# A hybrid decoder trunk on one core: five accumulator banks in its last gate, pool products by 64 by 64 blocks, and a new order of all instructions

## Chip, cores and metric

The kernel runs on one core of a Trainium2 chip. The metric is the device time of one execution in microseconds (us); less is better. A profile is one execution of the same program, taken by the hardware profiler. The engines are called as in the profile: PE (matrix products), PEld (its weight loads), DVE (vector), ACT (activations), POOL (GpSimd) and SP (which only issues DMAs here).

## What is computed

Two layers (L = 2) over 256 tokens and 1024 features, all in float32. `z` is split by columns among a convolution module, a pooling mixer, and a sparse attention that keeps 64 keys per query; each is multiplied by a SiLU gate. Then come an output projection, a residual, and an addition gated by a sigmoid. A last RMSNorm ends it.

```python
for i in range(DEPTH):
    n = rmsnorm(h, norm_g[i])
    z = n @ w_in[i] + b_in[i]
    ...
    ya = conv_module(c_val, c_glu, ...) * jax.nn.silu(c_gate)
    yb = pool_mixer(p_in, pool_w[i], pool_b[i], pool_scale[i]) * jax.nn.silu(p_gate)
    ...
    yc = sparse_attention(q, k, v, qi, ki, wi) * jax.nn.silu(a_gate)
    h = h + jnp.concatenate([ya, yb, yc], axis=-1) @ w_out[i]
    h = h + (p[i] @ ple_w[i]) * jax.nn.sigmoid(h @ ple_gate_w[i])
return rmsnorm(h, final_norm_g)
```

In the pooling mixer each of four groups of 64 channels is multiplied by its own 64 by 64 matrix: `jnp.einsum('bsgc,gcd->bsgd', d, w)`.

## The kernel before

**Products.** Features lie on the 128 partitions, tokens in the free dimension. Every large weight arrives by DMA in one of three buffers `raw` (1 MB each). ACT or DVE rounds it to `hi`, DVE or POOL subtracts to get `lo`, and a product is three passes on PE: hi times hi, hi times lo, lo times hi. The sum of eight such k-steps stays in a PSUM bank. There are eight banks of 512 columns; `bank()` hands out banks 0 to 2 in turn, `bank("att")` banks 4 to 7. Small products (index scores, attention, pooling, convolution's pointwise part) are taken in float32 directly.

**Order.** The program text only records operations, each with the engines that may do it. `Order.issue` then issues them in the order of the string `ORDER`: two characters per operation, which say which operation comes next and which engine takes it. `PORT` adds waits between a few operations of POOL and DVE. Each engine works through its own part of that order strictly in a row, SP its DMAs too. A PSUM bank counts as one cell: whoever writes any part of it waits for all that read or write it.

**Places of which the prediction speaks.** (1) In `rope_pair` the projected `z` has its partitions swapped by four DMAs `zs<-z`, issued by SP or ACT; the index scores (`score1`, products `bank<-qir`) need the result, and they need bank 5, which the projection Q0 of layer 1 uses until `rescale` (DVE) and `evac` (ACT) have emptied it. The load of `mt` (mats, 384 KB) stands in SP's queue too. (2) In the convolution's layer norm (`ln`), POOL takes `nyl`, the reciprocal root, DVE makes `nm` of it, and two `c<-bank,nm,nyl` normalise, after which PE transposes them. (3) In the pooling mixer two products by block-diagonal 128 by 128 matrices (`mt`) are made in each layer. (4) In `last_gate` the tokens lie on the partitions; the output of 256 by 1024 is made in five parts (`LAST_PARTS`). Parts 4 and 5 (columns 512 to 767 and 768 to 1023 of the second 128 tokens) share a bank. After a part's products come a sigmoid in place (ACT), the product with `ple` (DVE), the sum with the transposed residual `ht` (DVE), a square with its sum (ACT), and a small step of the variance `nv` (DVE). `ht` comes from PE transposes that ACT copies (`vt<-bank`).

```python
LAST_PARTS = ((0, 0, 512), (0, 512, 512), (1, 0, 512), (1, 512, 256), (1, 768, 256))
```

Of the kernel before, what the change touches and what calls it, by code (L numbers as in the profile page):

```python
# [20 lines left out]
L = 2  # L21
S = 256
# [41 lines left out]
    "#Z#m###j#&#*#p#-%y#0#K#3#N#6%|#9#d#_#Q#<#b#?#B#s#}$##v&##g$B#y$E#W$($3$*$H&*#T$K&&$6&-$Q%3%7&B$T$W$p%:$9&0(9%<"  # L64
    "$<$N$Z%@%B&Q&3$?$.&W%F&6$0#E#H%W%H$a%K$d&9%N&^%Z%R$g&<%_$j%T$s&d$^&?&j%a)3&E&p$v&v&K&H&|$y&N&T(<$m&Z$|)g&a(?%#"
    "&g)<*Q%&&m%*)6)?(B(E(H%d)9%g(K&s%j+<)p%m(N(Q%0&y)j)t%p%s(T(W%w)B(Z(&(#(^*Z(d)E(*(m*T)H*^(s)K(a*W)N(|)Q(-)m.^+?"
    ")T(p(3(0(y)W+C3p(j*a(6+E-s)Z3s*d)^3v*g(h+I3y(w*j)a3|4#*m.a4&*p4*/H*s)$4-40*v.e)v.g*y)y43)d46)|+#)&.j*#*&)*7p49"
    "+K).*|-v4<**+44?*-4B)14E*04H-z+-+N-|*3+0+Q4K+**94N+T*64Q*<+W.#/K%-+Z*B+(/N+^6g*@+a*F4T*I.&4W4Z.*+7+d.-4^+j+g4a"
    "*L.0/Q7g4d.34g6j*O.64j4m.m4p/U.94s.<,&.?,*,y+:8N4v,-,0,3+v-#4y,|,6+p,9/W6n.B4|+s6p,<.p5#,?-&.E5&.s.N.L,B6t.R5*"
    ".v,E.I5-.y--,H7s.|50,K.U9-/#53+n,N/&-*+z/Z/*/^,Q.X/0,T/a7y,W56/d+}8Q,Z6v59,^/-.[/g,a5<6y,d,$-06|,g-37#,j8U/6/:"  # L70
    "-6,m7&90/<5?7*-9/3,p/j,s-<,v/v-?94/y/|/m0&-B0*8^-E0-5B8a-H/@005E-K8d8W/C0#/p030B068g-N0E5H/F090H0<7--Q0?5K70-T"
# [992 lines left out]
```

## Time and profile before

| | us |
|---|---|
| median of 3 runs | 335.52 |
| the three runs | 335.54, 335.52, 333.81 |
| profiled execution, its own time | 334.27 |
| span from first to last instruction | 332.2 |
| PE busy in the span | 315.4 |
| DVE, ACT, POOL busy | 255.0, 181.2, 154.0 |

The profiled execution is 1.25 us under the median, and 2.1 us of it lie outside the span. In rows of the timeline the columns are start, duration, engine, line, operation, what it writes and reads, shapes and count; in brackets the idle time of the engine before it and what ended it. Consecutive equal instructions are merged, and their duration is then that of the row. A duration of a PE product runs past the start of the next one, since products are pipelined; the distance of starts says what one costs.

### The profile page before, as it was taken

What the parts mean: (1) busy time and instruction counts of PE and PEld (TensorE: products, weight loads), DVE (VectorE), ACT (ScalarE), POOL (GpSimd) and SP (SyncE); (2) the same over time, 40 slices, a digit from 0 to 9 for tenths busy, and PEclk for the clock granted to TensorE, in tenths of its full rate; (3) what the DMA queues carried; (4) which work ended last, traced back from release to release, by engine and by line L of the source; (5) the groups of instructions that cost most, each with busy time, mean ns of one, the idle gap of its engine ahead of it and who ended that gap; (6) DMA issues with size and microseconds to landing.
All of it is one profiled execution on the core that took longest, in us unless ns stands there. A gap on an engine that the chain in (4) does not pass through costs nothing. (4 is left out here: it accounts for less than half of the span.)

```text
span 332.2 us, 6467 instructions
## 1 busy us (share of the span) xinstructions
PE 315.4 (95%) x2468; PEld 294.1 (89%) x2469; DVE 255.0 (77%) x570; ACT 181.2 (55%) x319; POOL 154.0 (46%) x109
## 2 busy tenths in 40 slices
PE   8989999898999999999999998999999989999990
PEld 3979999797789999999999998998898979998870
DVE  3887999997786898357997987987798783838373
ACT  2776552628658545252686526536767661533463
POOL 1003577979985000461300463996967655020122
PEclk9999999999999999999999999999999999999997
DMA  7959977461163155626456774372343338351003
GB/s 214 325 190 357 303 271 240 156 228 36 33 247 134 52 202 195 269 77 221 161 144 247 272 236 149 129 257 94 128 132 131 118 117 280 134 215 80 0 0 126
DMA packets 13549, 57.31 MB, mean 173 GB/s; under 512 B 2128, under 2 KB 3280, under 8 KB 8016
## 3 DMA queue, kind: packets, MB, share of 16 engines
q1 hardware_dynamic: 12128, 55.14, 47.6%
q10 hardware_dynamic: 1392, 1.77, 1.8%
q8 instruction: 19, 0.31, 0.4%
q14 instruction: 10, 0.08, 0.1%
HBM read 52.45 MB, written 1.05 MB: 161 GB/s over the span
## 5 line engine op out<-in xcount | busy, mean ns | idle before, releaser
L209 PE MATMUL bank<-xhi,hi 128*128 128x256 f32 x464 | 132.0, 286 | 0.3 <-ACT ple L260 0.2
L209 PE MATMUL bank<-xlo,hi 128*128 128x256 f32 (+1 forms) x464 | 129.7, 281 | 0.5 <-DVE xlo L280 0.5
L209 PE MATMUL bank<-xhi,lo 128*128 128x256 f32 x448 | 125.9, 281 | 2.2 <-POOL lo L282 1.4
L282 POOL TENSOR_TENSOR lo<-raw,hi 128x1024 fp32r<-128x1024 f32 (+1 forms) x40 | 93.6, 2351 | 70.4 <-DVE hi L262 40.1
L260 ACT ACTIVATE hi<-raw 128x1024 fp32r<-128x1024 f32 (+2 forms) x89 | 87.3, 1007 | 54.1 <-PE bank L209 24.4
L209 PEld LDWEIGHTS bank<-xhi,hi 128*128 128x128 f32 x464 | 87.3, 188 | 1.8 <-ACT ple L260 0.4
L209 PEld LDWEIGHTS bank<-xlo,hi 128*128 128x128 f32 (+1 forms) x464 | 86.6, 187 | 1.1 <-DVE xlo L280 0.9
L209 PEld LDWEIGHTS bank<-xhi,lo 128*128 128x128 f32 x448 | 84.5, 189 | 2.8 <-POOL lo L282 1.8
L280 DVE TENSOR_TENSOR lo<-raw,hi 128x1024 fp32r<-128x1024 f32 (+2 forms) x58 | 64.9, 1147 | 9.5 <-ACT hi L260 9.2
L287 DVE SCALAR_TENSOR_TENSOR bank<-f,f,bank 128x256 f32<-128x256 f32 x116 | 55.9, 482 | 1.7
L209 PE MATMUL bank<-yhi,hi 128*128 128x256 f32 x128 | 36.3, 284 | 0.0
L209 PE MATMUL bank<-ylo,hi 128*128 128x256 f32 x128 | 36.1, 282 | 0.0
L209 PE MATMUL bank<-yhi,lo 128*128 128x256 f32 x128 | 35.9, 281 | 0.0
L209 PE MATMUL bank<-hi,xhi 128*128 128x256 f32 (+2 forms) x100 | 32.1, 321 | 0.7 <-DVE vt L270 0.7
L209 PE MATMUL bank<-hi,xlo 128*128 128x256 f32 (+2 forms) x100 | 31.3, 313 | 0.0
L209 PE MATMUL bank<-lo,xhi 128*128 128x256 f32 (+2 forms) x100 | 31.2, 312 | 0.0
L209 PEld LDWEIGHTS bank<-yhi,hi 128*128 128x128 f32 x128 | 24.1, 188 | 0.3 <-DVE c L229 0.2
L209 PEld LDWEIGHTS bank<-ylo,hi 128*128 128x128 f32 x128 | 24.1, 188 | 0.3
L209 PEld LDWEIGHTS bank<-yhi,lo 128*128 128x128 f32 x128 | 24.1, 188 | 0.0
L209 PEld LDWEIGHTS bank<-hi,xhi 128*128 128x128 f32 x100 | 18.8, 188 | 2.9 <-DVE vt L270 0.9
L228 ACT ACTIVATE z<-bank,f 128x256 f32<-128x256 f32 x21 | 9.3, 470 | 20.6 <-DMA zs<-z 9.2
L270 DVE TENSOR_TENSOR bank<-bank,rb 128x512 f32<-128x512 f32 (+1 forms) x26 | 17.3, 672 | 4.0 <-PE bank L209 3.8
(175 smaller groups left out, 470.2 us busy)
## 6 DMA issues: line engine op xcount, KB each, us to landing
raw<-in_w_in_dram SPq DMA_DIRECT2D x25, 1024.0 KB, 6.3
raw<-in_w_out_dram SPq DMA_DIRECT2D x8, 1024.0 KB, 4.8
raw<-in_w_gate_dram SPq DMA_DIRECT2D x8, 1024.0 KB, 5.0
raw<-in_w_v_dram SPq DMA_DIRECT2D x2, 1040.0 KB, 5.3
raw<-in_w_ple_dram SPq DMA_DIRECT2D x8, 256.0 KB, 5.2
zs<-z SPq DMA_DIRECT2D x21, 64.0 KB, 2.2
zs<-z ACTq DMA_DIRECT2D x19, 64.0 KB, 4.0
raw<-in_w_in_dram SPq DMA_DIRECT2D x4, 256.0 KB, 6.3
```

What stands on the lines that cost most here:

```text
L209: lambda: self.nc.tensor.matmul(o, lhsT, rhs, start=start, stop=stop, skip_group_check=True))],
L228: self.add([self.on_act(o, i, lambda: self.nc.scalar.activation(o, i, AF.Identity, bias=bias, **kw), len(ptr)), self.on_dve(o.free_size(), ...
L260: ways.append(self.on_act(o, i, lambda: self.nc.scalar.activation(o, i, AF.Copy)))
L270: ways.append(self.on_dve(n, lambda: self.nc.vector.tensor_tensor(o, a, b, op), late=late))
L280: ways.append(self.on_dve(n, lambda: self.nc.vector.tensor_tensor(o, a, hb, OP.subtract), late=late))
L282: ways.append(self.on_pool(n, lambda: self.nc.gpsimd.tensor_tensor(o, a, hb, OP.subtract)))
L287: self.add([self.on_dve(o.free_size(), lambda: self.nc.vector.scalar_tensor_tensor(o, a, s, b, op0=op0, op1=op1), len(ptr))], [a, b] + ptr ...
```

## The change

Three things. `last_gate` gets a fifth bank, and part 5 accumulates there; its first four k-steps are therefore also made by parts, so that the 512 columns of the second token half are two times 256. Its transposes take their buffers from a list of three banks. The pool products are four of 64 by 64 instead of two of 128 by 128 in each layer. And `ORDER` and `PORT` are replaced as a whole.

```diff
 ORDER = (
-    "#Z#m###j#&#*#p#-%y#0#K#3#N#6%|#9#d#_#Q#<#b#?#B#s#}$##v&##g$B#y$E#W$($3$*$H&*#T$K&&$6$-$Q%3%7&B$T$W$p%:$9&0(9%<"
...
+    "#m#Z###j#&#*#p#-%y#0#N#3#K#6#T#9#}#s$##^#Q#e#a#g%|$B#w$E#y$H$&&#$K#<$+#?&*#W$3$6#B&&$Q%3%7&B$9$O$p$T&-$<%K(9$W"
...
         ppl = bank("att")
         for j in range(2):
-            R.mm(ppl[:, j * S:(j + 1) * S], mt[:, 512 + j * 128:512 + j * 128 + 128], pd[j], start=(j == 0), stop=True)
+            for r in (slice(0, 64), slice(64, 128)):
+                c0 = 512 + j * 128 + r.start
+                R.mm(ppl[r, j * S:(j + 1) * S], mt[r, c0:c0 + 64], pd[j][r], start=(j == 0), stop=True)
...
-            return last_gate(hhi, hlo, ple, [banks[3], bank("att"), bank("att"), bank()])
+            return last_gate(hhi, hlo, ple, [banks[3], bank("att"), bank("att"), bank(), bank()])
...
+        tbs = [bank(), bank("att"), bank("att")]
         for a in range(2):
             for t in range(2):
                 R.tag = f"ht{a}{t}"
-                tb = bank("acc" if a == 0 else "att")
+                tb = tbs[(2 * a + t) % 3]
...
-        halves = ((0, 512), (512, 512))
-        order = [[(k, t, c, n) for k in range(GATE_OUTER) for t in range(2) for c, n in halves]]
+        order = [[(k, *part) for k in range(GATE_OUTER) for part in LAST_PARTS]]
+
+        def acc_of(t, c, n):
+            b, c0 = (accs[4], 768) if (t, c) == (1, 768) else (accs[2 * t + c // 512], c // 512 * 512)
+            return b[:, c - c0:c - c0 + n]
+
```

The new order, at the three places where the prediction uses it:

**The layer norm of layer 1.** DVE before, from the batch statistics of the convolution (`bmv`) to the second normalisation; `bank0` and `bank2` are gates of other branches, `yhi` and `ylo` a split for the output projection.

```order
L767 BN_AGGR bmv65_145<-bst64_144 128x2
L270 TENSOR_TENSOR bank0_61<-bank0_61,y078_158 128x512
L293 TENSOR_SCALAR vv66_146<-bmv65_145 128x2
L262 CAST yhi71_151<-bank0_61 128x512
L280 TENSOR_TENSOR ylo72_152<-bank0_61,yhi71_151 128x512
L287 SCALAR_TENSOR_TENSOR nm70_150<-bmv65_145,nyl67_147 128x2
L270 TENSOR_TENSOR bank2_63<-bank2_63,rb42_122 128x512
L229 TENSOR_SCALAR c269_149<-bank6_67,nyl67_147,nm70_150 128x256
```

And DVE in the changed program:

```order
L766 BN_AGGR bmv65_145<-bst64_144 128x2
L292 TENSOR_SCALAR vv66_146<-bmv65_145 128x2
L269 TENSOR_TENSOR bank0_61<-bank0_61,y078_158 128x512
L286 SCALAR_TENSOR_TENSOR nm70_150<-bmv65_145,nyl67_147 128x2
L261 CAST yhi71_151<-bank0_61 128x512
L279 TENSOR_TENSOR ylo72_152<-bank0_61,yhi71_151 128x512
L269 TENSOR_TENSOR bank2_63<-bank2_63,rb42_122 128x512
```

The step `vv` now stands ahead of the product in bank 0, and `nm` ahead of the split into `yhi` and `ylo`; the second normalisation has left DVE. ACT at the same place, before:

```order
L218 ACT_TABLE_LOAD
L218 ACTIVATE bank0_61<-bank0_61,f3_78 128x256 x2
L260 ACTIVATE hi20_100<-raw17_97 128x1024
L228 ACTIVATE c269_149<-bank6_67,nm70_150,nyl67_147 128x256
L218 ACTIVATE ag79_159<-bank2_63,f3_78 128x256 x2
```

And ACT in the changed program:

```order
L217 ACT_TABLE_LOAD
L217 ACTIVATE bank0_61<-bank0_61,f3_78 128x256 x2
L259 ACTIVATE hi19_99<-raw16_96 128x1024
L259 ACTIVATE hi20_100<-raw17_97 128x1024
L227 ACTIVATE c269_149<-bank6_67,nm70_150,nyl67_147 128x256 x2
L217 ACTIVATE ag79_159<-bank2_63,f3_78 128x256 x2
```

Another rounding (`hi19`) stands ahead of `hi20`, from which POOL subtracts next after `nyl`; both normalisations follow on ACT.

**SP's queue at the index scores of layer 1.** Before (`zs39<-z37` are the swaps for the index queries, `zs38<-z36` with 512 columns those of Q0, `raw` the weights):

```order
L312 DMA z36_116<-z36_116 64x256
L312 DMA zs38_118<-z36_116 32x256 x2
L312 DMA mt33_113<-in_mats_dram 128x768
L312 DMA raw15_95<-in_w_in_dram 128x2048
L312 DMA zs39_119<-z37_117 32x512 x2
L312 DMA raw17_97<-in_w_in_dram 128x2048
L312 DMA zs38_118<-z36_116 32x512 x2
L312 DMA raw16_96<-in_w_in_dram 128x2048
L312 DMA zs38_118<-z36_116 32x512 x2
```

And in the changed program:

```order
L311 DMA raw15_95<-in_w_in_dram 128x2048
L311 DMA zs39_119<-z37_117 32x512 x3
L311 DMA zs38_118<-z36_116 32x512 x2
L311 DMA raw17_97<-in_w_in_dram 128x2048
L311 DMA raw16_96<-in_w_in_dram 128x2048
L311 DMA zs38_118<-z36_116 32x512 x4
L311 DMA raw15_95<-in_w_in_dram 128x2048
L311 DMA zs39_119<-z37_117 32x512
L311 DMA mt33_113<-in_mats_dram 128x768
L311 DMA raw17_97<-in_w_in_dram 128x2048
```

The load of `mt` has moved from ahead of the index queries' swaps to behind many later ones, and the load of raw17 from ahead of Q0's swaps to behind them.

**The end of the last gate.** PE before, from the last products of part 4 (bank 2) over the last transposes (`f0<-f5`) to the first products of part 5, which has the same bank:

```order
L209 MATMUL bank2_63<-hi21_101,xhi34_114 128x256
L209 MATMUL bank2_63<-lo25_105,xhi34_114 128x256
L209 MATMUL bank2_63<-hi21_101,xlo35_115 128x256
L213 MATMUL bank5_66<-f0_69,f5_80 128x128 x3
L213 MATMUL bank1_62<-f0_69,f5_80 128x128 x4
L209 MATMUL bank2_63<-hi18_98,xhi34_114 128x256
L209 MATMUL bank2_63<-lo28_108,xhi34_114 128x256
L209 MATMUL bank2_63<-hi18_98,xlo35_115 128x256
```

And PE in the changed program, with part 5 in bank 0:

```order
L208 MATMUL bank2_63<-hi21_101,xhi34_114 128x256
L208 MATMUL bank2_63<-lo25_105,xhi34_114 128x256
L208 MATMUL bank2_63<-hi21_101,xlo35_115 128x256
L212 MATMUL bank1_62<-f0_69,f5_80 128x128 x4
L212 MATMUL bank4_65<-f0_69,f5_80 128x128 x3
L208 MATMUL bank0_61<-hi18_98,xhi34_114 128x256
L208 MATMUL bank0_61<-lo28_108,xhi34_114 128x256
L208 MATMUL bank0_61<-hi18_98,xlo35_115 128x256
L212 MATMUL bank4_65<-f0_69,f5_80 128x128
L208 MATMUL bank0_61<-hi19_99,xhi34_114 128x256
```

The seven transposes stand at the same place, an eighth has moved behind three products of part 5. ACT before, from the sigmoid of part 4 on:

```order
L218 ACTIVATE bank2_63<-bank2_63 128x256
L260 ACTIVATE vt45_125<-bank5_66 128x512
L260 ACTIVATE vt45_125<-bank1_62 128x512
L298 ACTIVATE q455_135<-q455_135,nyr082_162 128x512
L218 ACTIVATE pTs59_139,ssq80_160<-vt45_125 128x512
L218 ACTIVATE bank2_63<-bank2_63 128x256
L218 ACTIVATE pTs59_139,ssq80_160<-vt45_125 128x256
```

And ACT in the changed program:

```order
L217 ACTIVATE bank2_63<-bank2_63 128x256
L259 ACTIVATE vt45_125<-bank1_62 128x512
L259 ACTIVATE vt45_125<-bank4_65 128x512
L217 ACTIVATE bank0_61<-bank0_61 128x256
L217 ACTIVATE pTs59_139,ssq80_160<-vt45_125 128x512
L217 ACTIVATE pTs59_139,ssq80_160<-vt45_125 128x256 x2
```

The sigmoid of part 5 (bank 0) now stands ahead of the square of part 3 (`pTs,ssq<-vt`, 512 columns). On DVE the first step of `nv1` (which waits for that square) stands ahead of part 5's product with `ple` in both programs.

## Rows read from the trace of the kernel before

**Rows 1.** The page, busy time, share and instructions of each engine.

```profile
PE 315.4 (95%) x2468; PEld 294.1 (89%) x2469; DVE 255.0 (77%) x570; ACT 181.2 (55%) x319; POOL 154.0 (46%) x109
```

**Rows 2.** Waits of PE: releaser, us in total, times, longest.

```profile
PE bank L209 <- POOL qir L272: 1.2, 1, 1.2
PE bank L209 <- ACT z L228: 1.1, 1, 1.1
```

**Rows 3.** Timeline of SP, DVE and ACT before the index scores, layer 1.

```profile
192.81 0.53 SPq L312 DMA_DIRECT2D mt<-in_mats_dram  x1
195.24 1.15 SPq L312 DMA_DIRECT2D zs<-z  x2
...
201.13 0.69 DVE L270 TENSOR_TENSOR zs<-zs,f 128x512 f32<-128x512 f32 x1 [2.72 <-DMA zs<-z]
202.13 0.69 DVE L270 TENSOR_TENSOR bank<-bank,rb 128x512 f32<-128x512 f32 x1
...
202.86 0.84 ACT L228 ACTIVATE z<-bank,f 128x256 f32<-128x256 f32 x2 [0.66 <-DVE bank L270]
```

**Rows 4.** Timeline of DVE, POOL, ACT and PE at the layer norm, layer 1.

```profile
265.84 1.86 DVE L287 SCALAR_TENSOR_TENSOR nm<-bmv,nyl 128x2 f32<-128x2 f32 x1
...
265.28 2.39 POOL L282 TENSOR_TENSOR lo<-raw,hi 128x1024 fp32r<-128x1024 f32 x1
...
263.66 1.05 ACT L260 ACTIVATE hi<-raw 128x1024 fp32r<-128x1024 f32 x1
267.73 0.56 ACT L228 ACTIVATE c<-bank,nm,nyl 128x256 f32<-128x256 f32 x1 [3.02 <-DVE nm L287]
...
267.36 0.28 PE L209 MATMUL bank<-yhi,lo 128*128 128x256 f32 x1
268.35 0.33 PE L213 MATMUL bank<-f,c 128*128 128x128 f32 x1 [0.71 <-ACT c L228]
268.93 0.55 PE L213 MATMUL bank<-f,c 128*128 128x128 f32 x3 [0.25 <-DVE c L229]
```

**Rows 5.** Timeline of PE: pool products of layer 0, and products on half of the rows.

```profile
110.99 0.61 PE L209 MATMUL bank<-pd,mt 128*128 128x256 f32 x2
111.43 0.38 PE L209 MATMUL bank<-c,mt 128*128 128x256 f32 x1
...
86.95 1.14 PE L209 MATMUL bank<-zrk,zrq 64*128 64x256 f32 x8
88.02 0.44 PE L209 MATMUL bank<-pTs,vt 128*64 128x128 f32 x4
```

**Rows 6.** Timeline of PE, ACT and DVE at the end of the last gate.

```profile
321.27 0.93 PE L213 MATMUL bank<-f,f 128*128 128x128 f32 x7
322.91 0.39 PE L209 MATMUL bank<-hi,xhi 128*128 128x256 f32 x1 [0.71 <-DVE vt L270]
324.31 0.28 PE L209 MATMUL bank<-hi,xlo 128*128 128x256 f32 x1
...
323.64 0.64 ACT L218 ACTIVATE pTs<-vt 128x512 f32<-128x512 f32 x1
324.63 0.37 ACT L218 ACTIVATE bank<-bank 128x256 f32<-128x256 f32 x1 [0.26 <-PE bank L209]
...
324.40 0.15 DVE L293 TENSOR_SCALAR nv<-ssq 128x1 f32<-128x1 f32 x1
325.03 0.43 DVE L270 TENSOR_TENSOR bank<-bank,ple 128x256 f32<-128x256 f32 x1 [0.47 <-ACT bank L218]
```

**Rows 7.** Timeline of PE at the start: warm-up products, the first real ones, the last long wait.

```profile
1.25 4.88 PE L209 MATMUL bank<-f 128*128 128x512 bf16 x11 [1.25 <-DVE f L379]
6.03 0.58 PE L209 MATMUL bank<-phi,hi 128*128 128x256 f32 x1
6.41 0.42 PE L209 MATMUL bank<-plo,hi 128*128 128x256 f32 x1
...
21.98 0.38 PE L209 MATMUL bank<-xhi,lo 128*128 128x256 f32 x1 [0.76 <-DVE lo L280]
```

More of the change, by code (lines that the diff above doesn't have):

```diff
@@ new lines @@
+    "(s*a3p(j)W3s(g3v*d+E(a3y*g%-3|(w(d+I*j4#(n(p4&*m.a-s4**p4-(})Z40*s.e/H(z43+K46*v)v.g*y)$)y49)&)|)*.j*|*#+#*&4<"
+    "-v).4?**+44B*-4E*0)1-z+N+*-|*3+-+Q4H*6)a+04K+T+(4N+W/K4Q.#+Z*9+^*B*F/N.&*=6g*@.*4T+74W+a*I.-+d.04Z*L+g4^.3/Q4a"
+    ".64d*O)^.94g)d+j4j.<+:+m4m,*6p+s.?,&,-/U+v4p,|,0,34s.m,64v.E.p,9.B4y/W.L,<6t8T4|.R/Z7v,?6j5#.s,B5&.v.O,E6n+q.y"
+    ",H.I7m,K/^5*,N/a5-,Q.|+}9350,T/#53+z/&,W56,Z,y.X-&59-#,^-*6v/*.U6y,a/0-0--6|,d8W5<,$7#,g/--3,j7&8#.[-6/9,m/d/6"
+    "/45?,p/g8[/<7y-9,s/j-<96/v/y/|0#,v/m-?/C0&-B7*0*-E0-5B8d/@-H005E8g-K8^0B/F8j0E-N8m0H5H-Q8b5K0306090<-T7-5N0?-W"
@@ new lines @@
+    "700K5Q0^9:0N0Q0T0W0v0Z0|0y9<1&0a0d0g-Z0j1*0m0p1#-^1-239@5T290s-a105W13168p-d/s1B/p191<8s1E1?-g5Z;61H2?-j2E:Q5^"
+    "261K2<-m731N-q1Q8v7}1v2K5a1T1W8y2N5d1Z2Q9B1y5g2T795j1^761a8(2B5m2W2H1d1g1j5p1m2Z1p1s5s1|9E2^2a2#9H7=9d2s9K2v7@"
+    "2&2*7C5v5y2-5|6#8*6&;97L2y8-2|6*7F3#6-9N603&7N2d632g8|2j662m9Q2pAE207R9T3*693-807X:T3W30333639836<3=6?9W3[7T6B"
+    "7H6E3^3a:W3d3g9#3?3B3E3j3H3K3N3Q9g7Z3T6H3m6K867_6N899j6Q9&:Z7a7d9Z7g7j6T7s:^6W7p6Z9a9^6^9*<Z8<:99-8?9s9m8B9v90"
+    "8E:<9y8H9p6d:v6a:g;38K;v9|;<8N:#:?;?:&8Q:B:*:-:s:0:j;Z;B:3;#:6:a:d;z=m:m:p:E;&;|<^;0;*:y<$;-;K:H:|<(:L;E;Q:N;T"
@@ new lines @@
+    ";H;W;N;^<a>Q;p<<;a<e;j;m<h;d;s;g<6=v<?<*<-=p=y<9<0<3=s<B<E<NSd<W>U<Q<T>W<j<m<pAN<s?6<H=?=&?Q<K=B<v<y=E<|=9>[=*"
+    "=<=|=d=-=h=#=0=H=3>6=K>&>*AH=N=6>?=Q>B=j>3=T=Z>#?9>-=_>^>0>E??>g?U>HAT>9AQ=b><AW>N?W>K>m?Z>j?<>a>p>d>y=WAZ?*?B"
+    ">v?->|?^?#C*?&?m?EAh?pA^?sAj?vD0?yC9>s?|Ab@#Ae@&?H@g?K?N@j?a?d@m?g?j@r@*@Z@-BN@0@^AL?3?0@a@3Am@6BC@d@9BL@<B@Ap"
+    "@?@B@v@t@NBE@Q@y@EC-As@|AvBHBZBQBXA|C0C3B#@TC6B&@W@HA3B*AyBTE*D3@KCHC<D6B-CBC?CNB^CTCEA*A#B3B0A-B6A(E^A6FHCZA9"
+    "A0BgBaCKA<BeCQE4BjCWB9BmC^A?E.CaABEgCdE0CgE6D9CmBpBsCjBvByCsD<EaEjD?DBDECpEdB|C#CvC&IjDHFKC|DKDNE9DQD#CyFOE<DT"
@@ new lines @@
+    "D*D&DaE?DkOgDpFQEmD-I#OjEpDgDXFUOmD^DtEsOpDZEvOsDmOvEyImOyJTE|O|DeIqP#F#P&F&FWF*EBDyF-DvF0FZE#IsF9D|F^P*E(F3F7"
+    "P-FaF<F@P0FdJWP3FgIvI&FjFBFmP6FFEEFpEHP9FvI*FsEKF|G(ENJZFyR^G6I-G<EQG3G+P<G9EWGBIyG?I1I|G$GEP?J^J#GHJ&PBETGKJd"
+    "PEK?G.GNJ*PHPKJ-JbGQPNJ0PQJ3GTI3RgJ6G1I6GWRaGZI9PTG^EZI<ReJ<GaJ9JgPWKBJEGdPZH*JBH-GgH3H0J?H9GjKFI?H6P^JHGmIBSm"
+    "H<GpIEPaGsIHJLJjIKRkJmGvIQH?INPdJpGyITIXJsHBI_B<PgHEJvI[JOU*G|SpJyIbKNSvJ|RmH#KHHHJQRpHKK#RsIdK&H&KmHNIhKsKpKy"
+    "KvHQRvK|K7K0HTL#PjRyK3HWK+PmR|KLK-L&HZPpS#L9PsS&L<PvL?KQH^K:TKPyL*L-HaL0P|L3KTL6HdK=KWHgLBQ#HjKZQ&StLELHLKLNLT"
@@ new lines @@
+    "LQLmLsLpU3LyLWLZL^LaL|LdLgSzLjS*LvM#K^Q*M&HmKaHpS-Q-S0KdM9TNS4HsUZQ0S|M<TTHvT#Q3TQM?M*M-M0T&KjU-HyS6N*N-S9N0MB"
+    "H|N3Q6TXN6N<MmM3TZNBQ9M6NET*KgQ<NHQ?T-U^S=VHNKQBMEMHSBMKNNMNT^QEMQSFTaQHNQSHMpTdS?NTSNQKSLMTNWMWMZM^MaMdN9MgN?"
+    "MsNjMvMySQM|TgQNN#SUTjQQU1NmNpNZN^NaNsNdT0QTNvNgQWTmNyQZT3U7N|MjO#SWN&SZVKS^SaQ^O&U9QaVOW-ONQdO*OQO-O0U<O4SjTp"
+    "SgQgQjOTOWTsOZUbO^O6OaO9O<O?OBOEOHOKQmOdQpQsQvU?QyTvUBQ|TyR#VQUER&R*T|R-UHW0R0U$UKR3W4U&UNR6T6UQV^T9UWVmUTR9R<"
+    "R?V0RBVaREVWV3RHVZVTT<RKV6RNT?V9XQRQRTRWW*R[W6VvUeVyTBVpUhWBTEWEVsTHWQVjW<UjW9WmUmZHUpUsUvUyU|V#W?V&W&WZWqV*Wj"
@@ L939, in last_gate @@
             t, c, n = LAST_PARTS[i - 1]
[L940 removed]
+            o, r = acc_of(t, c, n), slice(c, c + n)
             R.tag = f"o{i}"
```

46 lines of the change are left out of this document (9 added, 37 removed).

## The prediction, made blind

> **What bounds it now.** I read the page first, for which engine sets the time, then the list of what that engine waits for, then the timeline at each wait. The page says that PE is busy for 95% of the span [rows 1], so the time is the sum of PE's products plus the moments in which PE stands still. What the change can take away is therefore either products or such moments. The list of PE's waits is short: besides the start, some ten of them, the longest 1.2 us or so [rows 2]. All of them together come to some 8 us: 332.2 of span less 315.4 busy is 16.8, of which 7.6 lie after PE's last product at 324.6 and 1.25 ahead of its first [rows 6, 7]. Each wait is then looked up in the timeline. Three are touched by the change in a way that the order of instructions lets one follow: the wait for the index scores in layer 1, that for the layer norm of layer 1, and that in the last gate. The others are moved too, but I cannot say to where.
>
> **The swaps before the index scores (layer 1).** PE stands for 1.1 us until ACT has emptied bank 5 [rows 2]. ACT's two evacuations start at 202.86, after DVE's rescale at 202.13. That one was ready earlier, but it stands in DVE's row behind the rotary product at 201.13, which waited 2.72 us for the swaps `zs<-z` [rows 3]. The swaps had been issued from 195.24 on and so took over 4 us, with the 384 KB of `mt` issued ahead of them at 192.81. In the new order that load is gone from there, and the 1 MB load that followed comes later. Lower bound of the gain: nothing, if the swaps are slow because of the weights that are left ahead of them. Upper: the whole wait, 1.1 us. I take 0.8, nearer to the upper end, because the rotary product waited more than twice as long for its swaps as PE waited for bank 5. The weight load that now stands behind Q0's swaps (that of P_IN) can't be asked for before Q0's `z` is there, 203.7 [rows 3]. I count nothing for it: its products stand some five k-steps later too, with four other projections ahead of them. If that cover is gone, PE waits for what the load is late beyond it.
>
> **The layer norm (layer 1).** PE's transposes of `c` begin at 268.35, where the product ahead began at 267.36; products of this size follow each other at 0.12, so 0.87 is lost there, and the two normalisations end one after the other, which costs 0.25 idle once more. ACT waited 3.02 us for `nm`, a step on 128 by 2 numbers that took 1.86 us. It began at 265.84 and ended when POOL's subtraction, begun at 265.28 and 2.39 long, ended [rows 4]: the two do not run together here, and the small step is held by the big one. In the new order `vv` stands earlier, `nm` follows it with nothing but one product between, and the rounding that POOL's next subtraction needs stands one rounding of 1.05 us later on ACT: it would end near 265.7. `nm` can be done by 265, before POOL holds it. Both normalisations then follow on ACT at 265.7 to 266.8, before PE comes there at 267.4. Gain: 0.9 to 1.3 us if `nm` gets ahead of the subtraction; nothing if it does not. I take 1.2, since three separate moves point the same way. What is late next: the products of the output projection, whose splits I find covered by the twelve products between.
>
> **The pool products.** Two full passes took 0.44 us (110.99 to 111.43), and a layer has four: 0.87. After the change a layer has eight passes on 64 rows. The nearest row is the attention's products on 64 rows with the same 256 columns: eight passes from 86.95 to 88.02, 1.07 us; they run in pairs, one on each half of the array, and lose something when the shape changes [rows 5]. So 0.2 more in each layer, 0.4 in both. If the two blocks do not pair, eight passes cost 8 by 0.217, 1.74, which is 0.87 more in a layer and 1.7 in both; if the shape change is hidden, nothing. I take 0.4: the trace shows pairs both for split rows and for split columns [rows 5], though not for both at once. This one goes straight into PE's sum. The Trainium skill, TensorEngine Tiling (Array Packing), section Theoretical Speedup, gives up to 2x where a dimension is 64 or less, by which the sum would be 0.9 better in both layers together; but here a full product already did two blocks at once, so the row decides. The same page, section Key Properties, says that a change of tiling mode drains the engine, and the 0.2 beyond four paired passes in the row agrees with it.
>
> **The last gate.** Twelve products of 512 columns become twenty-four of 256: at 0.13 a piece at most (twelve of part 5 start from 322.91 to 324.31) and two of these for one before, that is nothing, at most 0.1. PE's wait of 0.71 before part 5 disappears, since part 5 has a bank of its own [rows 6]. Seven transposes stand ahead of it as before, so its products start at about 322.1 and, with the eighth transpose, end some 0.7 earlier, by 323.9. What then sets the end is the row of ACT and DVE. ACT now does part 5's sigmoid (0.37) first and part 3's square (0.64) after it; DVE has to take the step `nv` of that square before it may multiply part 5. So: sigmoid to 324.3, square and the reading of its sum to some 325.1, `nv` 0.15, product from 325.25. Before, that product began at 325.03 [rows 6]. The gain of 0.7 on PE is spent on ACT, and I count plus 0.1 (from minus 0.7, were nothing in the way, to plus 0.3).
>
> **The start.** Its end is set by the weights of C_GLU: PE waits at 21.98 for their first half's `lo` [rows 7]. Their place in SP's queue, the fifteenth load, is the same in both orders, with the same bytes ahead. I count nothing; the cover is that PE stood still several times before.
>
> **The sum.** Minus 0.8, minus 1.2, plus 0.4, plus 0.1: minus 1.5. Against the profiled execution's 334.27 this is 332.8; against the median of the runs, which lies 1.25 higher, 334.0. I give the latter. It is 0.45% less; half a per cent, 1.7 us, is about what a measurement of this kernel can tell from no change, as its three runs themselves differ by that.
>
> **Rivals.**
>
> *The end gives too.* If ACT's sigmoid comes before the square has its input anyway, DVE isn't held, and the 0.7 of PE reaches the output: minus 2.2 to minus 2.3, 333.2. For it: the square waits for a copy of the eighth transpose, which may come late. Against: the order of DVE, which puts `nv` ahead.
>
> *The waits go elsewhere.* The whole order is new, and each wait that vanishes lets PE come sooner to the next producer. The index scores of layer 0 show it: PE waits there for POOL (1.2 us) [rows 2], and the order gives POOL the same rotary steps. Then pool products and last gate alone count: plus 0.5, and the time is 336.0.
>
> *Slower: the clock at the start.* Eleven warm-up products filled PE from 1.25 to 6.03, 0.43 each, the rate of the lower clock level for 512 columns, and the first real ones still followed at 0.38, where 0.12 is usual later [rows 7]. The new order has eight warm-up products there, which end at 4.7, and the first real product can't come before the input `p`, now loaded second, has been rounded: about 5.9. PE stands for 1.2 us. If the rise of the clock is put off by no more than that, three or four products cost 0.25 more each, hidden by later waits for weights. If it is put off by as long as it took before, nearly 5 us at 0.38 are 13 products that would else take 1.6, so 3.4 are lost; the waits up to 21.98 cover perhaps 1.5, and three more warm-up products among real ones take 0.7. That would add 2.6 and give 336.6, slower than before; it decides from about 3 us of lost work on. Against it: most of the idle time is short, and the products fed in between are there. The Trainium skill, TensorE: Matmul & The Clock Gate, section What's actually happening, has the array begin at half rate and rise after sustained activity; the trace agrees with the first half [rows 7], and no row shows a gap there.
>
> **How the numbers follow.** Forecast 0.5; the end gives too 0.15; waits elsewhere 0.2; the clock, or pool products that do not pair (plus 1.3, then 335.3 in all), 0.15. The time is that of the likeliest, 334.0. The low end takes all gains at their bounds (1.1, 1.3, 0.7) and no price for the pool products: 335.5 less 3.1 is 332.4, and 1 us less for the waits that I could not follow: 331.4. The high end is the clock case: 336.6. Faster by over half a per cent needs minus 1.7, which the forecast just misses and the second case passes; with the waits not followed, I give 0.42 for faster, 0.41 for the same and 0.17 for slower.
>
> **What would show it.** Right: in layer 1 `nm` takes under 0.5 us and ends before POOL's subtraction begins; PE has no wait for `c`, and under 0.7 for the index scores; eight pool passes in about 1.07; no wait ahead of part 5, and DVE's product of part 5 after the `nv` step near 3.8 us behind the last product of part 4. Wrong: a first real product at over 0.3 beyond 8 us, pool passes that start one after the other at 0.22, or new waits of PE over 1 us at places where it had none.

## The result, and the profile after

The changed kernel takes 337.72 us (median of 4 runs, 336.76 to 338.91) against 334.66 for the kernel before (4 runs, 332.58 to 335.54): a ratio of 1.0125, 95% interval 1.0077 to 1.0173 (the two medians alone give 1.0091). It is slower, by about 1%, and all four of its runs lie above the upper end of the predicted range (336.6). Here and below a ratio leaves out the runs that are over 1.5% above the fastest of their kernel, which were three of six in all_swaps_first and eight of twelve in second_place_only, so that the ratios of these two speak of their better runs alone; medians are of all runs. The profiled execution of the changed kernel took 336.76, 2.5 more than that of before; the span is 334.4.

First the table of stages of both kernels: per stretch its length, the busy time of PE, PEld, DVE, ACT and POOL with the number of instructions, the granted TensorE clock, the DMA's share and its rate in GB/s. The kernel before:

```profile
0.00:30.00 30.00, 26.98 (x177) 21.98 (x179) 20.32 (x38) 17.97 (x28) 3.12 (x13) 1.00 0.79 266
30.00:58.00 28.00, 28.00 (x239) 28.00 (x239) 26.24 (x45) 14.12 (x21) 19.09 (x12) 1.00 0.82 277
58.00:72.00 14.00, 12.84 (x107) 12.21 (x106) 13.72 (x36) 7.09 (x12) 13.92 (x9) 1.00 0.57 190
72.00:88.00 16.00, 14.78 (x112) 12.75 (x110) 12.40 (x51) 10.12 (x19) 14.24 (x10) 1.00 0.16 54
```

The changed kernel, and two shorter stretches of it below:

```profile
0.00:30.00 30.00, 24.63 (x179) 21.38 (x180) 19.67 (x35) 18.86 (x31) 2.92 (x12) 1.00 0.80 275
30.00:58.00 28.00, 27.84 (x235) 27.64 (x235) 26.21 (x46) 13.58 (x19) 17.11 (x10) 1.00 0.73 245
58.00:72.00 14.00, 10.68 (x65) 9.80 (x64) 10.52 (x22) 6.34 (x11) 10.89 (x6) 0.76 0.44 150
72.00:88.00 16.00, 13.95 (x116) 13.11 (x115) 13.57 (x52) 8.21 (x14) 11.72 (x9) 1.00 0.42 126
...
58.00:62.00 4.00, 0.99 (x9) 0.79 (x7) 3.67 (x8) 2.39 (x6) 2.28 (x2) 1.00 0.11 39
62.00:68.00 6.00, 5.68 (x25) 5.01 (x26) 2.88 (x8) 2.95 (x7) 6.00 (x4) 0.50 0.29 87
```

Read PE's counts (the first x). By 58 us both have done the same number of products, 416 and 414. From 58 to 72 the changed kernel does 65 where before did 107: 42 products at 0.12 each are 5 us, all lost in one place, and the granted clock, 1.00 everywhere else here, is 0.76 there. The rest of the program takes over half of it back (the spans differ by 2.2). The place is the index scores of layer 0. The timeline there after the change, of PE, POOL, ACT's queue and SP's in turn:

```profile
58.71 0.28 PE L208 MATMUL bank<-xhi,lo 128*128 128x256 f32 x1
62.32 2.15 PE L208 MATMUL bank<-qir 64*128 64x256 f32 x9 [3.32 <-POOL qir L271]
...
55.85 1.29 POOL L271 TENSOR_TENSOR qir<-z,f 128x512 f32<-128x512 f32 x1
59.65 1.27 POOL L271 TENSOR_TENSOR zs<-zs,f 128x512 f32<-128x512 f32 x1 [2.50 <-DMA zs<-z]
60.99 1.27 POOL L271 TENSOR_TENSOR qir<-qir,zs 128x512 f32<-128x512 f32 x1
...
52.90 2.05 ACTq L313 DMA_DIRECT2D zs<-z  x3
...
52.90 0.51 SPq L311 DMA_DIRECT2D zs<-z  x1
53.68 0.35 SPq L311 DMA_DIRECT2D raw<-in_w_in_dram  x1
```

The same place before, of PE, SP's queue and ACT's:

```profile
60.60 1.57 PE L209 MATMUL bank<-qir 64*128 64x256 f32 x14 [1.16 <-POOL qir L272]
...
54.17 0.51 SPq L312 DMA_DIRECT2D zs<-z  x1
54.79 0.52 SPq L312 DMA_DIRECT2D raw<-in_w_in_dram  x1
...
52.49 1.35 ACTq L314 DMA_DIRECT2D zs<-z  x2
```

PE waits 3.32 us for POOL where it waited 1.2 before [rows 2], and nine products behind the wait take 2.15 us where fourteen took 1.57. POOL itself stands 2.50 us, for swaps (`zs<-z`). These are the four swaps of the index query, three issued by ACT from 52.90 to 54.95 and one by SP, and in the midst of them, at 53.68, comes a 1 MB load of weights. Before, that load stood on SP's queue behind SP's last swap, and ACT's were out by then. From issue to landing (the last number, a median) ACT's swaps now take nearly as long as the load, which takes 5.4 us; SP's swap ahead of it does not:

```profile
zs<-z ACTq DMA_DIRECT2D x3, 64.0 KB, 5.1
zs<-z SPq DMA_DIRECT2D x1, 64.0 KB, 1.9
```

The two short stretches of the table above show what follows: 9 products in the four microseconds of the wait, and then six microseconds at a granted clock of 0.50. So there are two losses, one behind the other: 2.2 us more of standing still, and the time at 0.50, which is the 1.2 GHz level, where 25 products were done. The list of PE's waits after the change (releaser, total, times, longest) has a second one on POOL's rotary steps, for the first attention scores of layer 0, 2.05 at 83.88 and 1.05 in layer 1:

```profile
PE bank L208 <- POOL qir L271: 3.3, 1, 3.3
PE bank L208 <- POOL zrk L271: 3.1, 2, 2.1
PE bank L208 <- DVE xhi L261: 1.7, 1, 1.7
```

The places that the prediction followed, in timelines of the changed kernel: PE at the index scores of layer 1, the pool products, the layer norm's transposes, and the end of the last gate's part 4 with the transposes and the start of part 5 behind it; then DVE at the layer norm and at the end.

```profile
208.11 1.14 PE L208 MATMUL bank<-qir 64*128 64x256 f32 x8 [0.27 <-issue]
...
115.66 0.28 PE L208 MATMUL bank<-xhi,lo 128*128 128x256 f32 x1
115.87 1.08 PE L208 MATMUL bank<-pd,mt 64*64 64x256 f32 x8
116.88 1.99 PE L208 MATMUL bank<-c,mt 128*128 128x256 f32 x8
...
271.98 0.60 PE L212 MATMUL bank<-f,c 128*128 128x128 f32 x4
...
323.94 0.28 PE L208 MATMUL bank<-hi,xlo 128*128 128x256 f32 x1
324.06 0.93 PE L212 MATMUL bank<-f,f 128*128 128x128 f32 x7
324.74 0.36 PE L208 MATMUL bank<-hi,xhi 128*128 128x256 f32 x1
...
268.79 0.16 DVE L286 SCALAR_TENSOR_TENSOR nm<-bmv,nyl 128x2 f32<-128x2 f32 x1 [0.21 <-POOL nyl L431]
...
327.60 0.15 DVE L292 TENSOR_SCALAR nv<-ssq 128x1 f32<-128x1 f32 x1 [0.39 <-ACT pTs L217]
327.67 0.42 DVE L269 TENSOR_TENSOR bank<-bank,ple 128x256 f32<-128x256 f32 x1
```

No transposes of `c` wait any more [rows 4], none of part 5 either [rows 6], `nm` takes 0.16 instead of 1.86, and the index scores of layer 1 wait 0.27 instead of 1.1.

### The profile page after: what moved, and what is told of

It reads as the page before. It is cut to its first block, busy times and chain, and to the rows that moved or that the text cites. A ratio compares the mean times of both kernels' runs of the same rounds, so it can differ in the third digit from the quotient of the medians.

```text
span 334.4 us, 6493 instructions
## 1 busy us (share of the span) xinstructions
PE 314.1 (94%) x2489; PEld 295.6 (88%) x2489; DVE 262.6 (79%) x574; ACT 177.8 (53%) x319; POOL 147.6 (44%) x105
## 3 DMA queue, kind: packets, MB, share of 16 engines
HBM read 52.45 MB, written 1.05 MB: 160 GB/s over the span
## 4 chain that ended last, share of the span: by engine, by line
PE 67%; DMA 15%; DVE 5%; POOL 4%; ACT 3%; issue 2%; ACTq 2%; SPq 1%; POOLq 0%; DVEq 0%
PE bank L208 64%; DMA zs<-z 5%; DMA raw<-in_w_in_dram 5%; PE bank L212 3%; DMA raw<-in_w_v_dram 2%; DMA f<-in_sp_dram 2%; DVE lo L279 2%; POOL zrk L271 2%; ACTq L313 1%; POOL zs L271 1%; ACT hi L259 1%; DVE bank L286 1%; POOL zrq L271 1%; SPq L311 1%; POOL lo L281 1%
## 5 line engine op out<-in xcount | busy, mean ns | idle before, releaser
L259 ACT ACTIVATE hi<-raw 128x1024 fp32r<-128x1024 f32 (+2 forms) x81 | 80.4, 1013 | 60.2 <-PE bank L208 33.3
L281 POOL TENSOR_TENSOR lo<-raw,hi 128x1024 fp32r<-128x1024 f32 (+1 forms) x36 | 84.1, 2350 | 56.1 <-DVE hi L261 29.7
L279 DVE TENSOR_TENSOR lo<-raw,hi 128x1024 fp32r<-128x1024 f32 (+2 forms) x62 | 71.6, 1173 | 12.4 <-ACT hi L259 10.5
L208 PE MATMUL bank<-hi,xhi 128*128 128x256 f32 (+2 forms) x104 | 33.0, 317 | 0.0
L208 PE MATMUL bank<-lo,xhi 128*128 128x256 f32 (+2 forms) x104 | 32.3, 311 | 0.0
L208 PE MATMUL bank<-hi,xlo 128*128 128x256 f32 (+2 forms) x104 | 32.2, 309 | 0.0
L208 PEld LDWEIGHTS bank<-hi,xhi 128*128 128x128 f32 x104 | 20.0, 192 | 1.7 <-issue 0.7
```

What stands on the lines that cost most here:

```text
L208: lambda: self.nc.tensor.matmul(o, lhsT, rhs, start=start, stop=stop, skip_group_check=True))],
L259: ways.append(self.on_act(o, i, lambda: self.nc.scalar.activation(o, i, AF.Copy)))
L279: ways.append(self.on_dve(n, lambda: self.nc.vector.tensor_tensor(o, a, hb, OP.subtract), late=late))
L281: ways.append(self.on_pool(n, lambda: self.nc.gpsimd.tensor_tensor(o, a, hb, OP.subtract)))
```

## Experiments

Theory A: swaps that are asked for behind, or at the same time as, a 1 MB load land with it; POOL's rotary steps wait for them, PE for POOL; and behind a wait of that length the clock falls. Rivals: POOL's row is late by itself (its own work, or the waits on DVE that the new order gives it); or the loss is at the start, as the prediction's slow case had it. All runs are in one table; each ratio is to the kernel before on the same chip. A "stop" below is a place where PE waits; e 6 and e 7 are the two projections that follow the index query in layer 0.

| kernel | median, us | range | ratio, 95% interval |
|---|---|---|---|
| swaps_first | 335.28 | 332.31 to 338.63 | 1.0035 (1.0001 to 1.0069) |
| fill_wait | 337.58 | 333.86 to 338.98 | 1.0093 (1.0057 to 1.0130) |
| before_load_first | 335.34 | 333.91 to 337.32 | 1.0060 (1.0025 to 1.0095) |
| before_pool_blocks | 335.37 | 330.89 to 337.86 | 1.0010 (0.9971 to 1.0048) |
| all_swaps_first | 332.31 | 327.05 to 341.26 | 0.9840 (0.9798 to 0.9882) |
| second_place_only | 337.40 | 331.06 to 344.93 | 0.9955 (0.9922 to 0.9988) |
| before_swaps_first | 331.82 | 329.66 to 333.84 | 0.9947 (0.9919 to 0.9974) |
| mats_back_layer1 | 336.33 | one run | |
| psb_early | 328.06 | 325.32 to 329.42 | 0.9820 (0.9769 to 0.9870) |
| swaps_first_layer1 | 327.88 | 324.98 to 331.07 | 0.9795 (0.9736 to 0.9854) |
| wait_bare | 333.66 | 330.68 to 336.35 | 0.9998 (0.9963 to 1.0033) |
| wait_filled | 331.49 | 328.62 to 335.35 | 0.9941 (0.9913 to 0.9968) |

The kernel before had medians of 333.2 to 333.9 beside them.

**swaps_first.** The edit, as instructions of SP and ACT (`zs_119<-z_117` are the swaps of the index query, `raw_97` the load):

```diff
 SP   zs_119<-z_117 32x512
+SP   zs_119<-z_117 32x512
 SP   raw_97<-in_w_in_dram 128x2048
-ACT  zs_119<-z_117 32x512 x3
+ACT  zs_119<-z_117 32x512 x2
```

(The load also comes after ACT's two in the order that is written out.)

> The changed kernel with one thing moved: in layer 0 the 1 MB weight load that SP issues between the last swaps of the index query (QI) goes behind all four of them, and one of the swaps goes from ACT's queue to SP's, so that two stand on each. Theory (the load ahead of the swaps holds them, they hold POOL's rotary steps, and these hold PE's index scores of layer 0): the two late swaps land near 55.5 instead of 59.3; POOL's multiplication of them then waits only for its own row, and starts at 57.1 instead of 59.6; PE waits about 0.9 us instead of 3.3, and since that is short the granted clock stays at 1.00. That is 2.4 for the wait and about 2 for the clock, so 333.3 instead of 337.7 (332.5 to 334.5, as some of it may be waited away at the next stop). Rival (POOL's row is late by itself, or by the waits on DVE that the new order gives it): the wait stays at about 3.3 and the time at 337.7. Rival (the loss is at the start, where PE stands still between the warm-up products): the time stays within 0.5 of 337.7 as well, whatever the swaps do.

POOL's step begins at 56.98 with no wait, and PE's wait for the index scores is 0.27. The whole time falls by less than expected, though, since PE now stands longer at the next stop. The timeline of PE there, and of POOL ahead of it:

```profile
80.68 1.38 PE L206 MATMUL bank<-zrk,zrq 64*128 64x256 f32 x8 [4.45 <-POOL zrk L269]
...
60.82 7.16 POOL L279 TENSOR_TENSOR lo<-raw,hi 128x1024 fp32r<-128x1024 f32 x3
73.14 1.29 POOL L269 TENSOR_TENSOR zs<-zs,f 128x512 f32<-128x512 f32 x1 [5.16 <-issue]
...
79.32 1.31 POOL L269 TENSOR_TENSOR zrk<-zrk,zs 128x512 f32<-128x512 f32 x1
```

POOL's row stands 5.16 us ahead of its rotary steps. The profile names nothing that ended this wait; in the changed kernel POOL waits 4.81 us at the same place, and there it names the swaps. SP issued two 1 MB loads at 63.27 and 63.65, ACT five swaps from 62.82 on. It looks like the same picture at a second place, which all_swaps_first and psb_early test: in the new order two loads, not one, stand ahead of the swaps of the next two projections.

**fill_wait.** Bf16 products that nobody reads, ahead of the first index score, in the bank that it overwrites:

```diff
+if (t, l) == (1, 0):
+    for i in range(14):
+        R.mm(pbs[1], idle[:, :128], idle, start=True, stop=True)
 for hp in range(2):
```

> The changed kernel with 14 more bf16 products of 512 columns, which nobody reads, ahead of PE's first index score of layer 0, in the bank that this score overwrites. They keep PE busy for about 3 of the 3.3 us that it waits there; the wait for POOL itself stays, and the first score still starts near 62.2. Theory (the products behind the wait run at half rate because PE stood still so long that the granted clock fell to 0.50): with PE busy the clock stays at 1.00, the products behind follow at 0.12 instead of 0.2 to 0.24, and the time falls by about 2 us to 335.7 (335.2 to 336.2). Rival (they are slow for another reason, the weights or the traffic): nothing changes, 337.7, and the granted clock still shows a drop or the steps stay long.

The timeline of PE (which has 13 of the 14 products) shows that the first part of the forecast came out; the time, 337.58 against 335.7, did not. The ten products behind the filled wait took 1.35 us (nine took 2.15 in the changed kernel), and the clock stayed at 1.00:

```profile
58.08 2.97 PE L208 MATMUL bank<-f 128*128 128x512 bf16 x13
60.98 1.35 PE L208 MATMUL bank<-qir 64*128 64x256 f32 x10
```

But PE came to the second stop sooner, and waited 4.9 us there instead of 2.1; the granted clock was 0.50 behind that wait (84 to 88). What one stop gave, the next took.

**before_load_first.** SP's queue in the kernel before:

```diff
 SP   mt_113<-in_mats_dram 128x768
-SP   zs_119<-z_117 32x512
 SP   raw_97<-in_w_in_dram 128x2048
+SP   zs_119<-z_117 32x512
```

> The kernel before with one thing moved: in layer 0 the same 1 MB weight load goes ahead of the last swap of the index query on SP's queue, instead of behind it. Theory (a swap asked for behind a 1 MB load lands with the load): that swap lands near 60 instead of 57.7, POOL's rotary steps follow at 60 to 62.5, PE waits 3.3 us or more instead of 1.2, the granted clock falls behind it, and the time grows by 4 us, from 334.7 to 338.7 (337.5 to 340). Rival (the new order is slow there for another reason): the swap lands as before, 57.7, and the time stays within 1 us of 334.7.

PE's wait is that of the changed kernel, with the order of before all around it:

```profile
61.95 1.80 PE L206 MATMUL bank<-qir 64*128 64x256 f32 x6 [3.40 <-POOL qir L269]
```

The granted clock was 0.75 from 60 to 64. The time grew by 1.5 to 2 us, not 4: the wait of 1.2 at 79 for POOL's `lo` vanished, since PE came later. One load ahead of one swap is enough to make the wait; what it costs depends on the next stop too.

**second_place_only and all_swaps_first.** At the second place, SP's and ACT's queues (`zs_118` belongs to e 7):

```diff
 SP   zs_119<-z_117 32x512 x3
+SP   zs_119<-z_117 32x512
+SP   zs_118<-z_116 32x512 x2
 SP   raw_96<-in_w_in_dram 128x2048
 SP   raw_95<-in_w_in_dram 128x2048
-ACT  zs_118<-z_116 32x512 x4, zs_119<-z_117 32x512
+ACT  zs_118<-z_116 32x512 x2
```

all_swaps_first has this and the edit of swaps_first, second_place_only this alone.

> The changed kernel with the swaps of layer 0 ahead of the weight loads at both places: at the index query as in the first run, and at the next projections (e 6 and e 7), where two 1 MB loads that stood on SP's queue ahead of five swaps go behind them, and of the five two go from ACT's queue to SP's, and the last of e 6 too, from behind those of e 7. Theory (POOL's rotary steps, which PE waits for, wait for swaps that stand behind loads): the swaps land near 65 instead of 73.9, POOL's row runs on from 68 without its 5 us gap, its last step for the first attention scores ends near 75.6 instead of 80.6, and PE, which came there at 76 and waited 4.5 us, waits at most 1; the granted clock does not fall at 82 to 85. So 4.5 less for the wait and 1.5 to 2 for the clock, of which the next stops take back some: 329.5 to 331.5, against 335.3 with the first place alone and 333.9 before. Rival (POOL is late there by its own work or by its waits on DVE): the wait stays above 3 us and the time at 335. Rival (the loads, put 1 us later, become what PE waits for): the wait for POOL goes and waits for hi and lo of w0 4 and w0 2 take its place, 333 or more.

> The changed kernel with the swaps ahead of the loads at the second place alone (e 6 and e 7 of layer 0); at the index query the load stays ahead. Theory: PE waits 3.3 us for the index query as in the changed kernel and its granted clock falls to 0.50 behind it, but its wait of 2.05 us for the first attention scores goes: 337.7 less 2, about 335.7 (335 to 336.5). If the two places were one cause (the first lateness makes the second), nothing changes, 337.7.

Three of six runs of all_swaps_first lie at 327.05 to 328.98, below the forecast, as by theory A and against both rivals (none of the three was profiled; psb_early shows the rows). Four of the twelve of second_place_only lie at 331.06 to 332.78, and the one of these that was profiled (331.57) has a wait of 2.9 for the index query and none for the first attention scores of layer 0: the two places are two causes. But the other runs go up to 341 and 345, and the median of second_place_only, 337.40, lies above its forecast and only 0.3 below that of the changed kernel. The profiled execution of all_swaps_first is one of the long ones (341.26). Some 4 us of it are a wait that ends at 31.66, behind weights that came late. The rest is in the timeline of DVE and of POOL:

```profile
69.88 9.34 DVE L267 TENSOR_TENSOR psb<-f 128x2 f32<-128x2 f32 x1
...
64.55 7.18 POOL L279 TENSOR_TENSOR lo<-raw,hi 128x1024 fp32r<-128x1024 f32 x3
71.67 1.30 POOL L269 TENSOR_TENSOR zs<-zs,f 128x512 f32<-128x512 f32 x1
...
77.89 1.32 POOL L269 TENSOR_TENSOR zrk<-zrk,zs 128x512 f32<-128x512 f32 x1
```

`psb` is a product on two columns that takes 0.15 in other places, and POOL's row has no gap as long as it lasts: it ends at 79.22, when POOL's last rotary step does (77.89 plus 1.32). Behind it PE waited 3.9 us from 83 on for ACT's `z`, and 1.6 at 87 for POOL's `lo`; that both were late because DVE's row was is argued here, and tested by psb_early.

**psb_early.** The two-column step goes to another place in DVE's order:

```diff
+DVE  psb<-f 128x2                  (between the splits of weights, near 32)
 DVE  lo<-raw,hi 128x1024
 ...
-DVE  psb<-f 128x2                  (behind the first MAX8 of layer 0, near 70)
```

> The run with all swaps of layer 0 first, and one small step of DVE moved: psb, a product on 128 by 2 numbers, which stood on DVE's row at 70 beside POOL's rotary steps, goes to 33, where POOL stands still. In the profiled execution of all_swaps_first psb began at 69.88 and took 9.34 us; it ended at 79.2, with the last of POOL's eight steps that followed each other without a gap, and everything behind it on DVE's row was late: PE waited 3.9 us at 82.7 and 1.6 at 87.1, and the granted clock fell to 0.50. Theory (a small two-input step of DVE can't begin beside POOL's and gets in only where POOL pauses; the swaps, now early, took away the pauses): no run is over 332 any more, the median is 328 to 329, as the three undisturbed ones of all_swaps_first (327.05 to 328.98), and no step of DVE is longer than 3 us. Rival (those long runs have another cause): they come again, half of the runs at 333 to 341, and another step of DVE shows the long hold.

All six runs are under 330, as forecast, the step takes 0.16, and in the timeline POOL's rotary steps run from 67.20 to 74.73 without a gap:

```profile
67.20 1.29 POOL L269 TENSOR_TENSOR zs<-zs,f 128x512 f32<-128x512 f32 x1
...
73.44 1.29 POOL L269 TENSOR_TENSOR zrk<-zrk,zs 128x512 f32<-128x512 f32 x1
```

This version, the changed kernel with four swaps on the other queue, three loads behind them and one small step moved, is 1.8% faster than the kernel before (1.3 to 2.3%), and so beats both. Of second_place_only no long run was profiled; wait_bare below, which is the same with `psb` early, has none above 336.4, where second_place_only had eight of twelve.

**swaps_first_layer1.**

> As psb_early, and the same edit at one place of layer 1: the last two swaps of e 6, on ACT's queue behind the mixer's 384 KB and a 1 MB load, go ahead of both, one of them on SP's queue. Theory: they land near 222 instead of 226.7, POOL's row loses its gap of 3.9 us there, and PE's wait of 1.1 to 1.3 us for the first attention scores of layer 1 goes: 1 less than psb_early, 327 to 328. Rival (POOL's other steps, or the loads put later, come last there): no change against psb_early.

PE's wait for the first attention scores of layer 1, 1.0 in psb_early, is gone from its list; the medians (327.88 and 328.06) differ by less than these runs can tell.

**before_swaps_first.**

> The kernel before with the same edit: at the index query of layer 0 the swaps ahead of the mixer's matrices and the 1 MB load, at the next projections one 1 MB load behind the swaps of e 6 and e 7, and the last swap of e 6 on SP's queue. Theory: its wait of 1.16 us for the index query falls to 0.5 to 0.8, since POOL's own row comes next there, and the wait of 1.2 us at 79 for lo, a step on POOL that stands behind the rotary ones, falls to 0 to 0.5: 1 to 1.7 less, so 332.2 to 333 against 333.9. Rival (POOL's own row sets both waits): within 0.5 of 333.9.

The time fell by some 1.8 us, a little more than expected, but not by the waits named: in its profile (333.84, the longest of its runs) PE still waits 1.0 us for the index query and 0.9 for `lo`, 0.5 less together. Where the other 1.3 come from stays open.

**wait_bare and wait_filled.** The pair that measures the clock. Both have the load ahead at the index query, the second place mended and psb early; wait_filled has 12 of the products of fill_wait.

> The changed kernel with the swaps first at the second place (e 6 and e 7 of layer 0) and psb early; at the index query the load stays ahead of the swaps, so PE waits there about 3 us, and no later stop takes its lateness back. It is the bare half of a pair. Theory: the granted clock falls to 0.50 behind the wait, and the time is that of psb_early, 328.1, plus some 2 us more of wait and 2 of clock: 331.5 to 332.5, without the runs above 336 that second_place_only had. Rival (a wait costs its own length alone): 330.

> The other half: the same kernel with 12 bf16 products of 512 columns, which nobody reads, on PE in that wait; POOL's late step and the start of the first index score stay where they are. Theory (behind a wait of 3 us the products run at half rate, which the granted clock shows, and it is the standing still that brings it down): the clock stays at 1.00, the scores and the products behind them follow at full rate, and the time is 2 us less than that of wait_bare: 329.5 to 330.5. Rival (the filling changes nothing, the steps are long for another reason): the same time as wait_bare within 0.5.

The filling takes off 2.2 us by the medians (333.66 to 331.49), 1.9 by the ratios, where 2 was forecast; both lie some 1.5 higher than I had said. The table of stages of wait_bare has

```profile
56.00:60.00 4.00, 1.65 (x14) 1.44 (x14) 3.33 (x7) 3.05 (x6) 2.93 (x3) 0.94 0.00 1
60.00:66.00 6.00, 6.00 (x28) 5.31 (x28) 3.55 (x9) 3.28 (x6) 6.00 (x4) 0.50 0.35 85
```

and that of wait_filled (its longest run, 335.35), whose first score starts at 66.17,

```profile
66.00:72.00 6.00, 5.83 (x48) 5.50 (x49) 3.94 (x11) 3.79 (x6) 6.00 (x4) 1.00 0.33 79
```

28 products behind a bare wait of 2.35 us, 48 in the same time behind a filled one that left 1.83 us of standing still.

**mats_back_layer1 and before_pool_blocks** test two terms of the prediction by themselves: the changed kernel with one load moved back, and the kernel before with the pool blocks alone.

```diff
+SP   mt_113<-in_mats_dram            (ahead of the 1 MB load before layer 1's index query)
 SP   raw<-in_w_in_dram 128x2048
 ...
-SP   mt_113<-in_mats_dram            (behind the swaps of e 6)
```

> The changed kernel with the 384 KB load of the mixer's matrices of layer 1 back ahead of the 1 MB load that precedes the index query's swaps. It tests the first term of the prediction (minus 0.8): if the load's absence is what shortened PE's wait for the index scores of layer 1, the swaps land about 1 us later (near 205 instead of 204) and the wait, 0.27 in the changed kernel, is 1 to 1.3 again. If the two new loads' order made the gain, the wait stays under 0.5.

```profile
209.09 1.14 PE L206 MATMUL bank<-qir 64*128 64x256 f32 x8 [1.29 <-ACT z L225]
```

The wait is back, 1.29: the load's place made the gain of the first term. One run says nothing of the time.

> The kernel before with the pooling mixer's products of the 64 by 64 blocks alone, at the places where the two full products stood; nothing else is changed. By the prediction the eight passes of a layer pair and take about 1.07 us from first to last start with what follows, 0.2 more than before, plus 0.4 in all: 335.1 against 334.7. If they do not pair: plus 1.7, 336.4. If the change of shape costs nothing: no change.

The ratio agrees with plus 0.4, and excludes the unpaired case (1.7 us, 0.5%) only just. The rows of the changed kernel settle it: eight passes take as long as four pairs.

## Why the prediction was wrong

**The terms that I followed came out, within a microsecond.** The index scores of layer 1: minus 0.8 forecast, 0.27 of wait left of 1.1, so minus 0.8; the experiment with the load moved back shows that the cause was right. The layer norm: minus 1.2 forecast; the two idle times of 0.71 and 0.25 are gone [rows 4], minus 1.0. The pool products: plus 0.2 a layer forecast; first start to the next product's is 1.01 in layer 0, where two halves of 0.44 stood before [rows 5], and the change of shape costs 0.09 more ahead of them (115.66 to 115.87, where 0.12 is usual): plus 0.2 to 0.3. The last gate: plus 0.1 forecast (its own times, 325.25 against 325.03, give plus 0.2); from the first transpose ahead of part 5 to the end of the span it is 334.4 less 324.06, 10.3, where it was 332.2 less 321.27, 10.9 [rows 6]: minus 0.6. Its mechanism was right: DVE waits 0.39 us for the square before `nv`, and its product of part 5 came 3.73 us behind part 4's last product, near the 3.8 of the mark (before, 325.03 less 321.15, 3.88). What was off is the row behind it, 0.4 shorter (6.7 to the end, where it was 7.2), which I had held to be unchanged. All of that lies behind DVE's last scaling (it starts at 330.01, before at 327.38), in the transfers of the output, and from one profile each it may be luck. The rival "the end gives too" comes near in size, but DVE was held, so its mechanism isn't what happened. The start: nothing forecast, and by 30 us the changed kernel has done 179 products, the kernel before 177. Together that is minus 1.9, where I forecast minus 1.5.

**The step that failed is the one that left the other waits alone.** It said of them "The others are moved too, but I cannot say to where", and of the index scores of layer 0, in the second rival, that "the order gives POOL the same rotary steps". POOL's steps were indeed the same; their input was not. The rule by which I had costed layer 1 (a load ahead of swaps on the queue holds what waits for the swaps) was there to be applied to layer 0, where the order of SP and ACT shows the 1 MB load ahead of the last of ACT's swaps, and two loads ahead of the next five. The first of these places cost 5 us from 58 to 72, against a forecast of minus 1.5 for all others. The prediction's own sign of being wrong, new waits of PE over 1 us, is there: 2.05 at 83.88, besides one of 1.7 at the start. The Trainium skill, DMA: Bandwidth & Descriptors, section Issuing engines are not separate DMA queues, says that transfers started by different engines run on the same DMA engines and interleave. The trace agrees that another queue is no way round a load: ACT's 64 KB swaps took 5.1 us beside SP's load, and 2.3 in swaps_first, where the load comes behind them.

**And a wait was priced at its length.** In the sum and in the rivals a microsecond of waiting was a microsecond, except at the start. Behind waits of 2.35, 2.9, 3.3, 3.4, 4.45 and 4.9 us the rows show a granted clock of 0.50 for some 3 to 7 us, behind those of 1.2, 1.8 and 2.05 one of 1.00. It need not begin with the first product: in second_place_only (2.9) ten products followed at full rate first, and the 0.50 ran from 61.9 to 65.1. The pair of runs puts a price of 2 us on it. The rival of the clock had the right mechanism at the wrong place: at the start PE stood still for 1.2 us and 1.7 us, but its products follow each other at 0.12 from 6.56 on, and nothing was lost by 30 us. PE there, after the change:

```profile
6.56 0.28 PE L208 MATMUL bank<-phi,lo 128*128 128x256 f32 x1
6.67 0.28 PE L208 MATMUL bank<-phi,hi 128*128 128x256 f32 x1
```

**The second rival, that waits go elsewhere, was the right one to fear**, and fill_wait, swaps_first and before_load_first show it at work: a stop in front gives its time to the next stop of the same producer. It had 0.2 and a price of plus 0.5, because I counted the waits that vanish and no new ones.

## What to carry to other kernels

When an order is made anew, follow each small transfer that a chain of work waits for, on every queue: what large transfer is issued ahead of it or among it, at each place where the pattern recurs, not only where the old profile shows a wait. Put the small ones first; no wait of PE in psb_early is for the loads that stand behind them there, and the kernel, with one small step of DVE moved as well, gained 1.8%. Price a wait of the matrix engine by the rows behind it, too.

## What the runs showed of the hardware

A two-input step of DVE on 128 by 2 numbers, 0.15 us by itself, took 9.34 us beside seven steps of POOL that followed each other without a gap, and ended with the last of them. The Trainium skill, SBUF — State Buffer, section SBUF: two separate sides, says that the pair of ports which the two engines share is locked for a whole instruction and the other engine blocks; here the block lasted over seven instructions. It does not always: in the profile of second_place_only (331.57) the same step began with the last of POOL's `lo` steps and was through after 2.44 us, when that ended, though POOL's next step followed with no gap to be seen. DVE and POOL there:

```profile
66.39 2.44 DVE L267 TENSOR_TENSOR psb<-f 128x2 f32<-128x2 f32 x1
...
64.03 4.78 POOL L279 TENSOR_TENSOR lo<-raw,hi 128x1024 fp32r<-128x1024 f32 x2
68.77 1.28 POOL L269 TENSOR_TENSOR zs<-zs,f 128x512 f32<-128x512 f32 x1
```

In the changed kernel it took 2.37 us, beside one step of POOL, which then paused for its swaps; in these two the block lasted for one instruction, as the page has it. What decides whether the waiting step gets in between two of POOL's isn't shown. That it sometimes does and sometimes doesn't would fit runs of one kernel that lie 14 us apart, as those of second_place_only do, and that moving the step made the runs even fits too. So an engine that is helped to run without gaps can starve another, in some executions.
